# The first quarter of the MLP's up-projection as seven half-block products

## The chip, the core and the metric

The kernel runs on one core of a Trainium2 chip. The core has five engines with instruction queues of their own: TensorE (PE) multiplies matrices into PSUM, VectorE (DVE) and ScalarE (ACT) work elementwise, GpSimd (POOL) here mostly issues adding DMA transfers, and SyncE (SP) issues plain ones. The engines wait for one another by semaphores. The metric is the device time of one execution in microseconds; less is better.

## What is computed

The reference is a residual block: three token mixers on one normalised input, an output projection with a residual, and an MLP. Only the end of the output projection and the MLP matter here (512 tokens, 1024 channels, 4096 hidden channels, all float32):

```
x = x + mixed @ w_out[l]
u = _rmsnorm(x, g_mlp[l]) @ w_ff1[l]
x = x + jnp.square(jax.nn.relu(u)) @ w_ff2[l]
```

The hidden channels are worked off in four quarters of 1024. For each quarter the kernel makes the up-projection (1024 x 1024 weights), squares the positive part, and adds the down-projection of that quarter onto x.

## The kernel before

**Number format.** A product in float32 is made of three passes of a faster format. `w_pair` (L71) splits a block of weights of 128 x 1024 into a high part `whi` on ScalarE (L77) and a low part `wlo` on VectorE (L78), which is the block less the high part. There are four buffers of each, so four blocks can be held split. The other operand is split likewise. Each step is then three matmuls: high x high, high x low, low x high (L87 to L89, L170 to L172, L197 to L199).

**Two ways to multiply.** A plain product of a 1024 x 1024 block with 512 tokens is made of 8 output columns of 128, each of 8 k-steps with three matmuls 512 wide. The other way is a Strassen-like scheme: weights and activations are cut in halves in both directions, and seven products of half blocks are made in place of eight. For it, sums of half blocks are needed: those of the weights are made by adding DMA transfers (`w_more`, L204, issued by POOL) and by one add on VectorE (L1331); those of the activations by VectorE. The seven results are added up into the four quadrants of the output on ScalarE and VectorE. In the up-projection a half product is `product_f` (L186): two blocks of weights, 48 matmuls that are 256 wide. In the output and down-projections it is `product` (L161), with matmuls 512 wide.

**Before the change** the output projection (`out_proj`), the down-projections and quarters 1 to 3 of the up-projection (`ff1`) are made the second way, and quarter 0 (`ff1_0`) the first way, from an array of its own, `w_ff1a`, in the layout for columns.

**Where quarter 0 stands.** In `out_proj` the last product d is accompanied by the transposes of the first four tiles of x1 (`u_tile` 0 to 3). `u_tile` transposes 4 x 128x128 into a bank `tr` (two of these), then ScalarE makes the high part (L97), VectorE the low part (L98), and ScalarE a float32 copy U (L1149). Tiles 4 to 7 need the second half of x1, which is only whole when product d has been added on. `ff1_0` starts columns 0 and 1 on k-steps 0 to 3, does tiles 4 to 7 meanwhile, then goes on with the other k-steps and columns. Between them stands `u_forms` (L1169): the sums S3, S5, S6 and S4 of the activations and their splits, which quarters 1 to 3 use. `norm1` works out the scale of the norm, which is applied behind the down-projection. `end(0)` and `end(1)` load the first blocks of the down-projection and split its first operands.

**Order.** The program is written in one order, and a scheduler puts the instructions of each engine in a queue: the earliest in the program that is ready goes first. Buffers of one tag are given out in the order of the program. The tags that matter: `whi`/`wlo` (4 each), `raw` (3 blocks, loaded from the SP queue), `rq` (4 blocks: weights of the other scheme, and U), `h` (8 tiles, each as large as a block; in `out_proj` they hold the split operands `sp...`), `S` (one buffer), `mix` and `gate` (8 each), PSUM banks `pj` (2), `q4` (4), `tr` (2).

Of the kernel before, what the change touches and what calls it, by code (L numbers as in the profile page):

```python
# [8 lines left out]
F32 = mybir.dt.float32  # L9
# [3 lines left out]
ALU = mybir.AluOpType  # L13
# [21 lines left out]
@with_exitstack  # L35
def tile_block(ctx: ExitStack, tc: tile.TileContext, xT, x_, memT, mem_, small,
               w_sbqk, w_mlqk, w_vo, w_if, w_gate, w_kv,
               w_proj, w_out, w_ff1a, w_ff1, w_ff2, out_):
    nc = tc.nc
    act, dve, pe, pool = nc.scalar, nc.vector, nc.tensor, nc.gpsimd  # L40
    act.preload_act_table_set("natural_log_exp_and_others")
# [7 lines left out]
    def f32(ap):  # L49
        return ap.bitcast(F32)  # L50
# [17 lines left out]
    def mix(name="mix"):  # L68
        return hp.tile([P, T], F32, tag="mix", bufs=NK, name=name)

    def w_pair(raw, parts=1, before=lambda i: None):  # L71
        hi = wp.tile([P, W], F32R, tag="whi", bufs=4, name="whi")
        lo = wp.tile([P, W], F32R, tag="wlo", bufs=4, name="wlo")
        for i in range(parts):
            c = slice(i * W // parts, (i + 1) * W // parts)
            before(i)
            act.activation(out=hi[:, c], in_=raw[:, c], func=AF.Copy)  # L77
            dve.tensor_tensor(out=lo[:, c], in0=raw[:, c], in1=f32(hi[:, c]), op=ALU.subtract)  # L78
        return hi, lo

    def load_w(src):
# [4 lines left out]
    def mm3(out, lh, ll, rh, rl, start, stop):  # L86
        pe.matmul(out, lh, rh, start=start, stop=False)  # L87
        pe.matmul(out, lh, rl, start=False, stop=False)  # L88
        pe.matmul(out, ll, rh, start=False, stop=stop)  # L89
# [111 lines left out]
    def w_more(raws, w, fh, kh):  # L201

        for v in range(2):
            pool.dma_start(out=raws[v], in_=w[fh, 2 * kh + v], accum_op=ALU.add)  # L204

    def w_pairs(raws):
        return [w_pair(raw) for raw in raws]


    sm = cp.tile([P, NSM], F32, tag="sm", name="sm")  # L210
# [868 lines left out]
    def w_raw(w, fh, kh):  # L1079

        raws = [fpool.tile([P, W], F32, tag="rq", bufs=4, name="rq") for v in range(2)]
        for v in range(2):
            nc.sync.dma_start(out=raws[v], in_=w[fh, 2 * kh + v])
        return raws

    def w_raw2(w, fh, kh):

        raws = [wp.tile([P, W], F32, tag="raw", bufs=3, name="rq2") for v in range(2)]
        for v in range(2):
            nc.sync.dma_start(out=raws[v], in_=w[fh, 2 * kh + v])  # L1090
        return raws
# [35 lines left out]
    def x1_add(th, fh, src, op, final=False):  # L1127
        for j in range(2):
            i = 2 * th + j
            dve.tensor_tensor(out=x1[i][fh], in0=x1[i][fh], in1=src[j], op=op)  # L1130
            if final:
                sq = tmp("sq")
                act.activation(out=sq, in_=x1[i][fh], func=AF.Square, accum_out=ssq[:, fh, i:i + 1])
# [59 lines left out]

    def f_first(qt):

        F11 = w_raw(w_ff1[qt - 1], 0, 0)
        F3 = w_raw2(w_ff1[qt - 1], 1, 1)
        w_more(F3, w_ff1[qt - 1], 1, 0)
        first["F"] = F11, F3

    def out_proj():

        B11, B3, sp11, sp3 = (early[n] for n in ("B11", "B3", "sp11", "sp3"))
        a, c, d, b = [pj(), pj()], [q4(), q4()], [q4(), q4()], [tr(), tr()]
        w11 = w_pairs(B11)
        w3 = w_pairs(B3)

        product(a, sp11, w11, True, False)
        w_more(B11, w_out, 1, 0)
        S = stile("S5")  # L1210
# [24 lines left out]
        product(a, sp12, w21, False, True)  # L1235
        sp22 = s_of(1, 1)
        sp4 = s_form(S, ALU.subtract, lambda k: S[:, k], lambda k: mA(1, 0, k))
        w4 = w_pairs(B3)
        for j in range(2):
            dve.tensor_tensor(out=V[j], in0=V[j], in1=b[j], op=ALU.subtract)  # L1240

        product(c, sp22, w4, False, True)
        w22 = w_pairs(B22)
        x1_add(0, 0, a, ALU.add, True)
        x1_add(1, 0, V, ALU.add)

# [12 lines left out]
        act.activation(out=s, in_=o, func=AF.Relu, scale=scale)  # L1259
        act.activation(out=out, in_=s.rearrange("p (a b) -> p a b", a=2), func=AF.Square)  # L1260

    def ff1_plain(f, w, o, ks):
        hi, lo = w
        for k in ks:
            mm3(o, hi[:, k * P:(k + 1) * P], lo[:, k * P:(k + 1) * P], u[k][:, 0, :], u[k][:, 1, :],
                k == 0, k == NK - 1)

    def ff1_0(R, end):

        def out(f, o):  # L1270
            s = tmp("rs")
            act.activation(out=s, in_=o, func=AF.Relu)
            act.activation(out=R[f // 4][:, f % 4, :], in_=s, func=AF.Square)

        ws, os = [], []
        for f in range(2):
            ws.append(load_w(w_ff1a[f]))
            os.append(pj())
            ff1_plain(f, ws[f], os[f], range(4))
            u_tile(4 + 2 * f)  # L1280
            u_tile(5 + 2 * f)
        norm1()
        for f in range(2):
            ff1_plain(f, ws[f], os[f], range(4, NK))
            out(f, os[f])
        for f in range(2, NK):
            if f < 5:
                u_forms(f - 2)
            if f == 6:
                end(0)  # L1290
            o = q4()
            ff1_plain(f, load_w(w_ff1a[f]), o, range(NK))
            out(f, o)
        u_forms(3)
        return end(1)

    def ff1(qt, R, end):

        def out(th, fh, j, src, scale=1.0):
            relu2(R[fh][:, 2 * j:2 * j + 2, 2 * th * P:2 * (th + 1) * P], src, scale)  # L1300

        F11, F3 = first["F"]
        G = w_ff1[qt - 1]
        a, c, d, e = [pj(), pj()], [q4(), q4()], [q4(), q4()], [tr(), tr()]
        w11 = first["w11"]
        w3 = w_pairs(F3)

        product_f(a, us["A11"], w11, True, False)
        w_more(F11, G, 1, 0)
        F21 = w_raw2(G, 0, 1)  # L1310
        V = [mix("V1") for j in range(2)]
        X = [mix("X1") for j in range(2)]
        for j in range(2):
            act.activation(out=V[j], in_=a[j], func=AF.Copy)
        w5 = w_pairs(F11)

        product_f(c, us["S3"], w3, True, False)
        w_more(F11, G, 1, 1)
        w21 = w_pairs(F21)
        for j in range(2):  # L1320
            act.activation(out=X[j], in_=c[j], func=AF.Copy)

        product_f(d, us["S5"], w5, True, False)
        F22 = w_raw(G, 1, 1)
        w6 = w_pairs(F11)
        for j in range(2):
            dve.tensor_tensor(out=X[j], in0=X[j], in1=d[j], op=ALU.add)

        product_f(a, us["A12"], w21, False, True)
        for v in range(2):  # L1330
            dve.tensor_tensor(out=F11[v], in0=F11[v], in1=F21[v], op=ALU.add)  # L1331
        w4 = w_pairs(F11)
        for j in range(2):
            out(0, 0, j, a[j])

        product_f(e, us["S6"], w6, True, True)
        w22 = w_pairs(F22)
        for j in range(2):
            dve.tensor_tensor(out=V[j], in0=V[j], in1=e[j], op=ALU.subtract)
            dve.tensor_tensor(out=X[j], in0=X[j], in1=V[j], op=ALU.add)  # L1340
            out(1, 1, j, X[j], -1.0)

        product_f(c, us["A22"], w4, False, True)
        got = end(0)
        for j in range(2):
            t = tmp("fs")
            dve.tensor_tensor(out=t, in0=V[j], in1=c[j], op=ALU.add)
            out(1, 0, j, t)

        product_f(d, us["S4"], w22, False, True)  # L1350
        got += end(1)
        for j in range(2):
# [195 lines left out]
```

## Time and profile before

| what | value |
|---|---|
| median of three runs | 1114.66 us (1113.29 to 1115.28) |
| profiled execution, device time | 1113.77 us |
| its span, first to last instruction | 1112.0 us |
| granted TensorE clock | 1.0 of full speed throughout |
| stage of quarter 0, first transpose of x1 to first matmul of the down-projection | 785.12 to 835.92 us |
| quarter 1 of the up-projection, the other way | 874.00 to 914.04 us |

The profile is of one execution. A row of a group reads: line, engine, operation, what is written from what, shapes, count, then busy us and mean ns of one, then the idle time of the engine before these instructions and what ended it. A row of the timeline reads: start, duration, engine, line, operation, count, and in brackets the idle time before it with its cause. Durations of matmuls overlap, since they are pipelined: what one costs is the distance between starts. Device time and span differ by what lies before the first and after the last instruction, 1.77 us here.

### The profile page before, as it was taken

Reading aid. Unit: us, or ns where it says so; the run is one execution under the profiler, and the core shown is the slowest. Engines: PE = TensorE matmul, PEld = TensorE weight load, DVE = VectorE, ACT = ScalarE, POOL = GpSimd, SP = SyncE. Lnnn points to the kernel's source line nnn. Section 1 sums busy time; section 2 is a strip of 40 time slices with the busy share of each in tenths; the row PEclk is TensorE's granted clock in tenths of the full one; section 3 lists DMA queues with packets and bytes.
Section 4 is the critical chain, followed back from the end, with each engine's and each line's share of the span. In section 5 each row is a group of like instructions: output and inputs, shape, how many; then the busy total and the mean of one; then the engine's idle time right before and its main releaser. Section 6 shows DMA issues by size and latency. Waiting matters only on the chain.

```text
span 1112.0 us, 16472 instructions
## 1 busy us (share of the span) xinstructions
PE 1104.6 (99%) x6080; PEld 955.5 (86%) x6080; DVE 861.1 (77%) x1268; ACT 727.3 (65%) x1210; POOL 129.7 (12%) x229
## 2 busy tenths in 40 slices
PE   9999999999999999999999999999999999999998
PEld 6788889999987888888888888888788998998997
DVE  5899777778767867577978798679758588688698
ACT  6666664658557967677869678535856475485573
POOL 0112211321101000000000000000011101111110
PEclk9999999999999999999999999999999999999999
DMA  9978889874612242326434221755397868778774
GB/s 355 362 202 237 256 216 275 232 225 144 227 39 72 81 145 74 110 85 208 148 94 138 80 93 58 209 140 126 115 245 164 213 185 218 177 201 223 175 186 114
DMA packets 62680, 190.31 MB, mean 171 GB/s; under 512 B 6788, under 2 KB 13572, under 8 KB 62600
## 3 DMA queue, kind: packets, MB, share of 16 engines
q1 hardware_dynamic: 46024, 131.38, 34.6%
q0 software_dynamic: 16288, 57.68, 25.3%
q8 instruction: 48, 0.79, 0.3%
q10 hardware_dynamic: 288, 0.20, 0.1%
q14 instruction: 32, 0.26, 0.1%
HBM read 172.45 MB, written 16.79 MB: 170 GB/s over the span
## 4 chain that ended last, share of the span: by engine, by line
PE 92%; DVE 3%; ACT 3%; DMA 1%; issue 1%; POOL 0%; ACTq 0%; DVEq 0%
PE pj L87 9%; PE pj L88 9%; PE pj L89 9%; PE q L170 5%; PE q L172 5%; PE q L171 5%; PE q L197 4%; PE q L198 4%; PE q L199 4%; PE q L87 3%; PE q L88 3%; PE q L89 3%; PE pj L171 3%; PE pj L170 3%; PE pj L172 3%; PE pj L198 2%
## 5 line engine op out<-in xcount | busy, mean ns | idle before, releaser
L77 ACT ACTIVATE whi<-rq 128x1024 fp32r<-128x1024 f32 x112 | 118.0, 1057 | 112.1 <-PE q L172 27.9
L78 DVE TENSOR_TENSOR wlo<-rq,whi 128x1024 fp32r<-128x1024 f32 x112 | 136.5, 1221 | 57.4 <-ACT whi L77 53.8
L77 ACT ACTIVATE whi<-B 128x1024 fp32r<-128x1024 f32 x84 | 88.6, 1058 | 74.8 <-PE q L198 16.5
L78 DVE TENSOR_TENSOR wlo<-B,whi 128x1024 fp32r<-128x1024 f32 x84 | 102.5, 1223 | 42.0 <-ACT whi L77 41.7
L87 PE MATMUL pj<-h,whi 128*128 128x512 f32 x304 | 120.8, 398 | 0.0
L89 PE MATMUL pj<-h,wlo 128*128 128x512 f32 x304 | 119.1, 392 | 0.0
L88 PE MATMUL pj<-h,whi 128*128 128x512 f32 x304 | 119.0, 391 | 0.0
L78 DVE TENSOR_TENSOR wlo<-raw,whi 128x1024 fp32r<-128x1024 f32 x72 | 87.9, 1221 | 33.9 <-ACT whi L77 33.6
L77 ACT ACTIVATE whi<-raw 128x1024 fp32r<-128x1024 f32 x72 | 75.9, 1055 | 47.8 <-PE pj L88 34.8
L170 PE MATMUL q<-whi,shi 128*128 128x512 f32 (+1 forms) x232 | 89.9, 388 | 0.0
L172 PE MATMUL q<-whi,slo 128*128 128x512 f32 (+1 forms) x232 | 89.8, 387 | 0.0
L171 PE MATMUL q<-wlo,shi 128*128 128x512 f32 (+1 forms) x232 | 89.8, 387 | 0.0
L204 POOL DMA_DIRECT2D rq<-in_w_ff_dram x50 | 43.0, 897 | 283.3 <-DVE wlo L78 160.0
L87 PE MATMUL pj<-y,whi 128*128 128x512 f32 x192 | 75.7, 394 | 0.0
L89 PE MATMUL pj<-y,wlo 128*128 128x512 f32 x192 | 75.0, 391 | 0.0
L88 PE MATMUL pj<-y,whi 128*128 128x512 f32 x192 | 74.9, 390 | 0.0
L89 PEld LDWEIGHTS pj<-h,wlo 128*128 128x128 f32 x304 | 57.1, 188 | 11.9
L87 PEld LDWEIGHTS pj<-h,whi 128*128 128x128 f32 x304 | 57.1, 188 | 10.9
L88 PEld LDWEIGHTS pj<-h,whi 128*128 128x128 f32 x304 | 57.2, 188 | 10.8
L172 PEld LDWEIGHTS q<-whi,slo 128*128 128x128 f32 x232 | 43.6, 188 | 8.9
L171 PEld LDWEIGHTS q<-wlo,shi 128*128 128x128 f32 x232 | 43.6, 188 | 8.9
L170 PEld LDWEIGHTS q<-whi,shi 128*128 128x128 f32 x232 | 43.6, 188 | 8.8
(443 smaller groups left out, 3220.8 us busy)
## 6 DMA issues: line engine op xcount, KB each, us to landing
rq<-in_w_ff_dram SPq DMA_DIRECT2D x56, 512.0 KB, 5.4
rq<-in_w_ff_dram POOLq DMA_DIRECT2D x50, 512.0 KB, 5.7
B<-in_w_vo_dram SPq DMA_DIRECT2D x48, 512.0 KB, 5.9
B<-in_w_vo_dram POOLq DMA_DIRECT2D x24, 512.0 KB, 6.9
raw<-in_w_proj_dram SPq DMA_DIRECT2D x24, 512.0 KB, 3.5
raw<-in_w_sbqk_dram SPq DMA_DIRECT2D x16, 512.0 KB, 3.9
raw<-in_w_mlqk_dram SPq DMA_DIRECT2D x16, 512.0 KB, 3.5
rawk<-in_w_kv_dram SPq DMA_DIRECT2D x14, 512.0 KB, 8.2
```

Source lines behind the costliest of these rows:

```text
L77: act.activation(out=hi[:, c], in_=raw[:, c], func=AF.Copy)
L78: dve.tensor_tensor(out=lo[:, c], in0=raw[:, c], in1=f32(hi[:, c]), op=ALU.subtract)
L87: pe.matmul(out, lh, rh, start=start, stop=False)
L88: pe.matmul(out, lh, rl, start=False, stop=False)
L89: pe.matmul(out, ll, rh, start=False, stop=stop)
L170: pe.matmul(o[:, c], lh, w[0][:, cw], start=st, stop=False, **mm)
L171: pe.matmul(o[:, c], lh, w[1][:, cw], start=False, stop=False, **mm)
L172: pe.matmul(o[:, c], ll, w[0][:, cw], start=False, stop=sp_, **mm)
L197: pe.matmul(o, wh, uh, start=start and k == 0 and f % 2 == 0, stop=False, **mm)
L198: pe.matmul(o, wh, ul, start=False, stop=False, **mm)
L199: pe.matmul(o, wl, uh, start=False, stop=stop and k == 3, **mm)
L204: pool.dma_start(out=raws[v], in_=w[fh, 2 * kh + v], accum_op=ALU.add)
```

## The change

`ff1_0` is written anew in the second way, with seven products in this order: 1 (bank a, weights w11, tokens' first half, u tiles 0 to 3), 2 (onto a, w21, tiles 4 to 7), 3 (c, w3 with S3), 4 (d, w5 with S5), 5 (onto c, w4, the four-fold sum of weights), 6 (e, w6 with S6), 7 (onto d, w22 with S4). Tiles 4 to 7 are transposed behind product 1. The results are put together in V and X, two copies of a and two of c on ScalarE, ten adds on VectorE. All low parts are made on VectorE (the new parameter `low` keeps its default).

The weights come from `w_ff1[0]`, which now holds all four quarters (so the index of the others moves by one). `first_loads`, called in `out_proj` behind the split of its last block, issues most loads: F4, F3 and F21 into tiles of tag `h`, F11 into `raw`, and the adding transfers on POOL in the order of use. F22 is loaded into `h` in `ff1_0`, and a last addition onto F11 is issued there. `w_ff1a` and `ff1_plain` are gone.

```diff
+    def first_loads():
+        G = w_ff1[0]
+        def half(fh, kh):
+            raws = [hp.tile([P, W], F32, tag="h", bufs=NK, name="hq") for v in range(2)]
+            for v in range(2):
+                nc.sync.dma_start(out=raws[v], in_=G[fh, 2 * kh + v])
+            return raws
+        F4 = half(0, 1)
+        w_more(F4, G, 0, 0)
+        F11 = w_raw2(G, 0, 0)
+        F3 = half(1, 1)
+        w_more(F3, G, 1, 0)
+        F21 = half(0, 1)
+        w_more(F4, G, 1, 0)
+        w11 = w_pairs(F11)
+        w_more(F11, G, 1, 0)
+        w_more(F4, G, 1, 1)
+        first["F"] = w11, F11, F4, F21, F3, lambda: half(1, 1)
...
         product(c, sp22, w4, False, True)
         w22 = w_pairs(B22)
+        first_loads()
...
     def ff1_0(R, end):
-        ws, os = [], []
-        for f in range(2):
-            ws.append(load_w(w_ff1a[f]))
-            os.append(pj())
-            ff1_plain(f, ws[f], os[f], range(4))
-            u_tile(4 + 2 * f)
-            u_tile(5 + 2 * f)
-        norm1()
-        for f in range(2):
-            ff1_plain(f, ws[f], os[f], range(4, NK))
-            out(f, os[f])
-        for f in range(2, NK):
-            if f < 5:
-                u_forms(f - 2)
-            if f == 6:
-                end(0)
-            o = q4()
-            ff1_plain(f, load_w(w_ff1a[f]), o, range(NK))
-            out(f, o)
-        u_forms(3)
-        return end(1)
+        w11, F11, F4, F21, F3, more = first["F"]
+        a, c, d = [pj(), pj()], [q4(), q4()], [q4(), q4()]
+        product_f(a, u_of(0, 0), w11, True, False)
+        for f in range(4, NK):
+            u_tile(f)
+        V = [mix("V1") for j in range(2)]
+        X = [mix("X1") for j in range(2)]
+        for j in range(2):
+            act.activation(out=V[j], in_=a[j], func=AF.Copy)
+        w21 = w_pairs(F21)
+        F22 = more()
+        product_f(a, u_of(1, 0), w21, False, True)
+        u_forms(0)
+        w3 = w_pairs(F3)
+        norm1()
+        for j in range(2):
+            out(0, 0, j, a[j])
+        product_f(c, us["S3"], w3, True, False)
+        u_forms(1)
+        w5 = w_pairs(F11)
+        w_more(F11, G, 1, 1)
+        for j in range(2):
+            act.activation(out=X[j], in_=c[j], func=AF.Copy)
+        product_f(d, us["S5"], w5, True, False)
+        w4 = w_pairs(F4)
+        u_forms(2)
+        product_f(c, u_of(1, 1), w4, False, True)
+        w6 = w_pairs(F11)
+        for j in range(2):
+            dve.tensor_tensor(out=X[j], in0=X[j], in1=d[j], op=ALU.add)
+        w22 = w_pairs(F22)
+        e = [tr(), tr()]
+        product_f(e, us["S6"], w6, True, True)
+        u_forms(3)
+        end(0)
+        for j in range(2):
+            dve.tensor_tensor(out=V[j], in0=V[j], in1=e[j], op=ALU.subtract)
+            t = tmp("fs")
+            dve.tensor_tensor(out=t, in0=V[j], in1=c[j], op=ALU.add)
+            out(1, 0, j, t)
+            dve.tensor_tensor(out=X[j], in0=X[j], in1=V[j], op=ALU.add)
+            out(1, 1, j, X[j], -1.0)
+        product_f(d, us["S4"], w22, False, True)
+        got = end(1)
+        for j in range(2):
+            t = tmp("fs")
+            dve.tensor_tensor(out=t, in0=V[j], in1=d[j], op=ALU.add)
+            out(0, 1, j, t, -1.0)
+        return got
```

More of the change, by code (lines that the diff above doesn't have):

```diff
@@ L37, in tile_block @@
                w_sbqk, w_mlqk, w_vo, w_if, w_gate, w_kv,
-               w_proj, w_out, w_ff1a, w_ff1, w_ff2, out_):
+               w_proj, w_out, w_ff1, w_ff2, out_):
     nc = tc.nc
@@ L69, in mix, with w_pair @@
         return hp.tile([P, T], F32, tag="mix", bufs=NK, name=name)
-    def w_pair(raw, parts=1, before=lambda i: None):
+    def w_pair(raw, parts=1, before=lambda i: None, low=dve):
         hi = wp.tile([P, W], F32R, tag="whi", bufs=4, name="whi")
@@ L77, in w_pair @@
             act.activation(out=hi[:, c], in_=raw[:, c], func=AF.Copy)
-            dve.tensor_tensor(out=lo[:, c], in0=raw[:, c], in1=f32(hi[:, c]), op=ALU.subtract)
+            low.tensor_tensor(out=lo[:, c], in0=raw[:, c], in1=f32(hi[:, c]), op=ALU.subtract)
         return hi, lo
@@ L204, in w_more, with w_pairs @@
             pool.dma_start(out=raws[v], in_=w[fh, 2 * kh + v], accum_op=ALU.add)
-    def w_pairs(raws):
-        return [w_pair(raw) for raw in raws]
+    def w_pairs(raws, low=dve):
+        return [w_pair(raw, low=low) for raw in raws]
     sm = cp.tile([P, NSM], F32, tag="sm", name="sm")
@@ L1194, in f_first @@
     def f_first(qt):
-        F11 = w_raw(w_ff1[qt - 1], 0, 0)
-        F3 = w_raw2(w_ff1[qt - 1], 1, 1)
-        w_more(F3, w_ff1[qt - 1], 1, 0)
+        F11 = w_raw(w_ff1[qt], 0, 0)
+        F3 = w_raw2(w_ff1[qt], 1, 1)
+        w_more(F3, w_ff1[qt], 1, 0)
         first["F"] = F11, F3
+    def first_loads():
[16 more added lines that the diff above has]
+        first["F"] = w11, F11, F4, F21, F3, lambda: half(1, 1)
     def out_proj():
@@ L1260, in relu2, with out @@
         act.activation(out=out, in_=s.rearrange("p (a b) -> p a b", a=2), func=AF.Square)
[L1262 to L1266, printed above, removed]
-    def ff1_0(R, end):
[L1270 to L1273, printed above, removed]
-        ws, os = [], []
-        for f in range(2):
-            ws.append(load_w(w_ff1a[f]))
-            os.append(pj())
-            ff1_plain(f, ws[f], os[f], range(4))
-            u_tile(4 + 2 * f)
-            u_tile(5 + 2 * f)
-        norm1()
-        for f in range(2):
-            ff1_plain(f, ws[f], os[f], range(4, NK))
-            out(f, os[f])
-        for f in range(2, NK):
-            if f < 5:
-                u_forms(f - 2)
-            if f == 6:
-                end(0)
-            o = q4()
-            ff1_plain(f, load_w(w_ff1a[f]), o, range(NK))
-            out(f, o)
-        u_forms(3)
-        return end(1)
+    def ff1_0(R, end):
+        def out(th, fh, j, src, scale=1.0):
+            relu2(R[fh][:, 2 * j:2 * j + 2, 2 * th * P:2 * (th + 1) * P], src, scale)
+        w11, F11, F4, F21, F3, more = first["F"]
+        G = w_ff1[0]
+        a, c, d = [pj(), pj()], [q4(), q4()], [q4(), q4()]
[11 more added lines that the diff above has]
+        w3 = w_pairs(F3)
+        norm1()
+        for j in range(2):
[16 more added lines that the diff above has]
+        product_f(e, us["S6"], w6, True, True)
+        u_forms(3)
+        end(0)
[13 more added lines that the diff above has]
+        return got
@@ L1302, in ff1 @@
         F11, F3 = first["F"]
-        G = w_ff1[qt - 1]
+        G = w_ff1[qt]
         a, c, d, e = [pj(), pj()], [q4(), q4()], [q4(), q4()], [tr(), tr()]
@@ L1534 @@
         "w_out": wide(a["w_out"][0]),
-        "w_ff1a": cols(a["w_ff1"][0][:, :D])[0],
-        "w_ff1": np.stack([wide(a["w_ff1"][0][:, i:i + D]) for i in range(D, 4 * D, D)]),
+        "w_ff1": np.stack([wide(a["w_ff1"][0][:, i:i + D]) for i in range(0, 4 * D, D)]),
         "w_ff2": np.stack([wide(a["w_ff2"][0][i:i + D]) for i in range(0, 4 * D, D)]),
```

## The prediction

> **What bounds the kernel now.** I read the page from the top, then the stage that the change touches. The page's first part and its chain of work say whether TensorE sets the time.
>
> ```profile
> span 1112.0 us, 16472 instructions
> PE 1104.6 (99%) x6080; PEld 955.5 (86%) x6080; DVE 861.1 (77%) x1268; ACT 727.3 (65%) x1210; POOL 129.7 (12%) x229
> PEclk9999999999999999999999999999999999999999
> PE 92%; DVE 3%; ACT 3%; DMA 1%; issue 1%; POOL 0%; ACTq 0%; DVEq 0%
> ```
>
> The chain is 92% matmul, at a granted clock that never drops. So a change pays by the matmul time that it takes off TensorE's stream, less the idle time that it opens there. Over the whole span VectorE is at 77% and ScalarE at 65%, but these are averages, so I cut out the stage. Its borders are found in the timeline of TensorE (columns: start us, us, engine, line, operation): first transpose of x1, first matmul of the plain quarter, first matmul of the down-projection.
>
> ```profile
> 785.12 1.03 PE L1145 MATMUL tr<-ident,x 128*128 128x128 f32 x8
> 785.91 0.48 PE L170 MATMUL q<-whi,shi 128*128 128x512 f32 x1
> ...
> 788.72 0.39 PE L87 MATMUL pj<-x1g,whi 128*128 128x512 f32 x1
> ...
> 803.50 0.39 PE L88 MATMUL q<-x1g,whi 128*128 128x512 f32 x1
> ...
> 835.92 0.39 PE L170 MATMUL pj<-whi,shi 128*128 128x512 f32 x1
> ```
>
> The view by windows has a row for each part, and the last one is the same work done in the new way: quarter 1, which already runs as seven half-block products (first matmul at 874.00, the next stage's at 914.04).
>
> ```profile
> 785.12:788.72 3.60, 3.60 (x21) 3.13 (x20) 2.27 (x3) 2.56 (x4) 0.00 (x0) 1.00 0.51 158
> 788.72:803.50 14.78, 14.77 (x74) 11.32 (x73) 11.77 (x24) 13.94 (x28) 0.00 (x0) 1.00 0.22 70
> 803.50:835.92 32.42, 32.42 (x145) 26.85 (x143) 18.06 (x20) 18.88 (x29) 4.32 (x5) 1.00 0.85 226
> 874.00:914.04 40.04, 40.04 (x337) 40.04 (x336) 27.35 (x29) 25.31 (x32) 5.13 (x6) 1.00 0.76 188
> 785.00:836.00 51.00, 50.99 (x239) 41.40 (x238) 32.10 (x45) 35.46 (x59) 4.32 (x5) 1.00 0.64 176
> 846.00:860.00 14.00, 14.00 (x64) 11.59 (x63) 13.93 (x15) 7.50 (x8) 2.58 (x3) 1.00 0.93 193
> ...
> 874.00 0.28 PE L197 MATMUL pj<-x1g,whi 128*128 128x256 f32 x1
> ...
> 914.04 0.40 PE L170 MATMUL pj<-whi,shi 128*128 128x512 f32 x1
> ```
>
> Columns: window, us, then busy us and instructions of PE, weight load, VectorE, ScalarE, POOL, clock, DMA share, GB/s. From 803.50 on TensorE is the limit, with VectorE and ScalarE at 56% and 58%. In the 14.78 us before that ScalarE is busy 13.94, or 94%: there the transposed tiles are drained, split and copied. That is the place to watch.
>
> **The matmul stream.** Removed: 8 columns x 8 k x 3 = 192 matmuls 512 wide. From 803.50 to 835.92 143 of them take 32.42, 0.2267 us each, so 192 are 43.53 us. Added: 7 products x 48 = 336 matmuls 256 wide; the quarter-1 row shows 336 in 40.04 us, 0.1192 each. Difference: **-3.49 us**. Half the width costs more than half the time (0.1192 against 0.1133), so of the eighth that seven products save in columns, 5.4 us, over a third is lost. The 32 transposes stay; eight take 0.79 us (785.12 to 785.91), 0.099 each.
>
> The page "TensorE: Matmul & The Clock Gate" of the Trainium skill, section Back-to-back issue gap, speaks against the change: in a stream of weight load and matmul pairs the spacing is set by both, about 81 ns at 128 columns and 131 ns at 512. On a straight line between these, an estimate from that page, 256 columns cost 98 ns, and 336 x 98 - 192 x 131 is a loss of 7.7 us. The trace does not agree: 227 ns at 512, 119 ns at 256, a gain of 3.5.
>
> **The start of the stage.** Before, 788.72 to 803.50 holds 49 matmuls (11.11) and 24 transposes (2.37), so 1.30 us are idle. After, the same place holds products 1 and 2 (96 x 0.1192 = 11.44) and the same transposes: 13.81, which would end at 802.53. Product 1 needs u tiles 0 to 3 only, product 2 needs 4 to 7, product 3 the split difference S3 and the pair w3. Before, TensorE could also work on columns whose pairs were all converted in advance, as four buffers hold four columns; now four buffers hold two products. What ScalarE did last there, and what it now has to do in addition:
>
> ```profile
> 771.51 0.39 PE L170 MATMUL pj<-whi,shi 128*128 128x512 f32 x1
> ...
> 782.39 0.39 PE L170 MATMUL q<-whi,shi 128*128 128x512 f32 x1
> ...
> 785.36 1.06 ACT L77 ACTIVATE whi<-raw 128x1024 fp32r<-128x1024 f32 x1 [0.44 <-ACT sq L1133]
> ...
> 800.87 1.35 ACT L1149 ACTIVATE U<-tr,sm 128x512 f32<-128x512 f32 x2 [0.24 <-DVE x1g L98]
> 802.34 1.06 ACT L77 ACTIVATE whi<-raw 128x1024 fp32r<-128x1024 f32 x1
> ...
> L1314 ACT ACTIVATE V<-pj 128x512 f32<-128x512 f32 x2 | 1.2, 588 | 0.5 <-PE pj L199 0.5
> ...
> L1260 ACT ACTIVATE R<-rs 128x512 f32<-128x512 f32 x8 | 4.9, 622 | 0.1
> L1340 DVE TENSOR_TENSOR X<-X,V 128x512 f32<-128x512 f32 x2 | 1.3, 682 | 0.0
> ...
> L1149 ACT ACTIVATE U<-tr,sm 128x512 f32<-128x512 f32 x8 | 5.4, 693 | 1.0 <-DVE x1g L98 1.0
> L78 DVE TENSOR_TENSOR wlo<-raw,whi 128x1024 fp32r<-128x1024 f32 x6 | 7.3, 1223 | 3.9 <-ACT whi L77 3.8
> ...
> L197 PEld LDWEIGHTS pj<-x1g,whi 128*128 128x128 f32 x96 | 18.4, 191 | 0.1
> L204 POOL DMA_DIRECT2D rq<-in_w_ff_dram x50 | 43.0, 897 | 283.3 <-DVE wlo L78 160.0
> ...
> rq<-in_w_ff_dram SPq DMA_DIRECT2D x56, 512.0 KB, 5.4
> rq<-in_w_ff_dram POOLq DMA_DIRECT2D x50, 512.0 KB, 5.7
> ```
>
> ScalarE's queue ends with the last U copies at 802.22; the conversion at 802.34 is that of column 4 and falls away. New before product 3: (a) two copies V of product 1's banks, 2 x 0.59 = 1.18; product 2 adds onto these banks, so it must wait for them. (b) Block w21 is loaded into tiles of tag h, and its two are released only when product c of the output projection is done (product d's first matmul, 782.39). With 5.4 us to landing that is 787.8, so the slot at 785.36, in which column 2 was converted, stays empty, and one conversion of 1.06 moves into the full stretch. (c) The first w3 conversion, 1.06. Together 3.30 us: 802.22 + 3.30 = 805.5 for w3's high part, and 1.22 later, 806.7, VectorE has the low part, which the third matmul of product 3 reads. Some of the 0.84 us that ScalarE idles in that stretch can be filled. Bounds: no delay beyond the 1.30 before, if the copies and conversions slip into gaps; or all of it, product 3 at 806.5. I take **805.9**, nearer the upper bound, as ScalarE is already at 94%. That is 3.4 us idle against 1.30, **+2.1 us**.
>
> Behind the V copies in ScalarE's queue stand the drains of u tiles 6 and 7, which product 2's second half reads; that wait is inside the 3.4. If x1 or a transposed tile comes later by t, all of this moves by t.
>
> **Products 3 to 7.** 240 x 0.1192 = 28.61. ScalarE has some 26 us to do in these 29 (eleven conversions, the splits of S5, S6, S4, A11, two X copies, six outputs of two passes) and VectorE some 25. The tightest is product 4: after 805.5 ScalarE does the second w3 half, the two outputs of bank a (4 x 0.6, as L1260), the S5 split and a w5 half, 1.06 + 2.4 + 1.06 + 1.06, so the high part at 811.1 and the low at 812.3, where product 4 is due at 805.9 + 5.72 = 811.6. I count **+0.3 us**; below is 0, above 1.5 if VectorE is late too. Products 5 to 7 have 2 us and more. Into the down-projection VectorE has S3, its split and w3's low parts to do within the first product; quarters 1 to 3 do the same at their ends, and no idle time of TensorE stands at 914.04. Zero, with +1.5 as the upper end.
>
> **Transfers.** Per 512 KB the queue rows give 1.54 us of all DMA engines for a plain transfer and 2.56 for an adding one:
>
> ```profile
> q1 hardware_dynamic: 46024, 131.38, 34.6%
> q0 software_dynamic: 16288, 57.68, 25.3%
> ```
>
> (0.524/131.38 x 0.346 x 1112, and likewise.) Removed are 8 plain ones (12.3 us), added 10 plain and 12 adding (46.1), over 768 to 820, a stretch whose DMA share was 0.51, then 0.22, then 0.85 with the down-projection's loads in it. It fits. The longest chain, block F4 with three additions, begins at about 771.5, when product b ends (product a's first matmul, 771.51), and takes 5.4 + 3 x 5.7 = 22.5: 794 alone, needed at 813. POOL's queue holds the additions in the order in which their products come, and was empty there (no POOL work in either window up to 803.50). The last addition onto F11 follows w5's low part (812.3): 0.9 to issue (L204), 5.7 to land, 819, two conversion steps, 821; product 6 is due at 823.4. Zero, and 2 us if landing doubles.
>
> **Sum.** -3.49 + 2.1 + 0.3 = **-1.1 us**. The profiled execution took 1113.77 (its span 1112.0 and 1.77 around it), so 1112.7 there; the median of the three runs is 0.9 above it, and against that I predict 1113.6.
>
> **The rivals.**
> - *The start is hidden.* ScalarE fits copies and conversions into gaps, idle time stays at 1.30: the whole 3.49 is gained, **1111.2**. For it: the U copies waited 1.0 us for VectorE's low part of the same tile, time that a conversion can use. Against: 94%.
> - *VectorE becomes the bound* (the other side). In 785 to 836 it works 32.10; six more low parts (6 x 1.22, as L78) and ten adds of 0.68 (as L1340) make 46.2, since all low parts lie on VectorE. With nothing idle that is less than the stage. The stage now is 50.80, so it decides from an occupancy of 91% down: at 85%, as each low part waits for its high part first, 54.4, +3.6, **1118.3**. For it: in 788.72 to 803.50 VectorE reached 80%. Against: at 846 to 860 it reached 13.93 of 14.
> - *Late blocks.* w21 or the last F11 lands 2 to 3 us later because the queue is fuller: the gain is eaten, **1115**.
> - *The narrow matmuls do not stream.* The change would then not do what it says. If each waited for its own weight load (L197, 191 ns), 336 would take 64.2 us, +20.7, **1135**. The row of 40.04 with 336 loads in it speaks against it. By the rule of the Trainium skill's page named above it would be 1114.66 + 7.7, some 1122, an estimate.
>
> **How the numbers follow.** Forecast 0.50 (own range 1112.2 to 1115.2), hidden start 0.24, VectorE 0.17, late blocks 0.07, narrow matmuls 0.02. A measurement of this kernel can tell about 0.2%, 2.2 us, from no change: faster means below 1112.4, slower above 1116.9. Faster: 0.22 of the hidden start and 0.06 of the forecast. Slower: 0.15 of VectorE, 0.01 of late blocks, 0.02 of narrow matmuls. The range leaves out the slower end of VectorE and the best end of the hidden start (which with fewer waits than before could reach 1110.5): 1110.8 to 1117.8.
>
> **What would show it.** Right: 336 more matmuls of 256 columns with starts 0.119 apart; idle time of PE's weight load in the first 18 us of the stage, ended by ScalarE or VectorE, summing to about 3; product 3 near 805.9 and the down-projection 1.1 us nearer to the first transpose. Wrong: waits of the weight load on low parts (L78) in products 4 to 7 (VectorE), conversions waiting for DMA (late blocks), or a gap before the down-projection.

## The result, and the profile after

| | before | after |
|---|---|---|
| median (range, runs) | 1114.22 us (1113.29 to 1115.34, 6) | 1123.59 us (1121.87 to 1126.31, 6) |
| ratio, 95% interval | | 1.0085 (1.0071 to 1.0099) |
| profiled execution, its span | 1113.77, 1112.0 | 1121.87, 1120.1 |
| stage of quarter 0 | 785.12 to 835.92, 50.80 us | 784.83 to 842.42, 57.59 us |

The change makes the kernel slower by 9.4 us, beyond the upper end of the range. The page of the changed kernel, its parts on busy time, clock and chain:

```profile
span 1120.1 us, 16822 instructions
PE 1104.2 (99%) x6224; PEld 963.1 (86%) x6224; DVE 873.3 (78%) x1284; ACT 733.8 (66%) x1220; POOL 140.1 (13%) x241
PEclk9999999999999999999999999999899999999999
PE 90%; DVE 4%; ACT 3%; DMA 2%; issue 1%; POOL 0%; SPq 0%; ACTq 0%; DVEq 0%
```

TensorE is as busy as before (1104.2 us against 1104.6), the span is 8.1 longer, and the clock row, 9 in every slice before, has an 8 in one slice. The view by windows shows the stage in three pieces and then quarter 1 (window, us, busy us and instructions of PE, weight load, VectorE, ScalarE, POOL, then clock, DMA share, GB/s):

```profile
784.83:795.37 10.54, 3.77 (x21) 2.94 (x19) 3.82 (x5) 4.03 (x9) 5.25 (x6) 0.89 1.05 311
795.37:812.10 16.73, 15.70 (x108) 14.91 (x109) 12.14 (x17) 15.11 (x28) 1.70 (x2) 0.86 1.06 230
812.10:842.42 30.32, 30.32 (x254) 30.32 (x254) 26.96 (x39) 22.21 (x34) 5.96 (x7) 1.00 0.92 220
880.53:920.83 40.30, 40.30 (x338) 40.30 (x336) 27.39 (x29) 25.32 (x32) 5.11 (x6) 1.00 0.74 183
```

In the first 10.54 us TensorE works 3.77, and VectorE and ScalarE some 4: they wait, while the DMA engines are full (1.05). From 812.10 to the down-projection TensorE has no pause. The last row is a second, small loss: quarter 1 takes 40.30 where it took 40.04, and quarters 2 and 3 likewise. The timeline of the changed kernel tells what was waited for. ScalarE:

```profile
785.93 1.24 ACT L97 ACTIVATE x1g<-tr,sm 128x512 fp32r<-128x512 f32 x2
793.69 1.06 ACT L77 ACTIVATE whi<-hq 128x1024 fp32r<-128x1024 f32 x1 [6.51 <-DMA hq<-in_w_ff_dram]
794.65 1.25 ACT L1149 ACTIVATE U<-tr,sm 128x512 f32<-128x512 f32 x2
```

TensorE:

```profile
795.37 1.97 PE L1145 MATMUL tr<-ident,x 128*128 128x128 f32 x8 [6.77 <-ACT U L1149]
```

SyncE's issues (four of 512 KB; the first two, at 782.08, are block F21 for w21, the others, at 788.41, F22), and VectorE's low parts of u tiles 0 and 1:

```profile
782.08 7.19 SPq L1208 DMA_DIRECT2D hq<-in_w_ff_dram  x4
```

```profile
786.63 1.41 DVE L98 SCALAR_TENSOR_TENSOR x1g<-tr,sm,x1g 128x512 fp32r<-128x512 f32 x2 [0.57 <-ACT x1g L97]
```

These are to be read from the last to the first. Transposes of u tiles 2 and 3 need the two banks `tr`, which the U copies of tiles 0 and 1 set free. The high parts of these tiles were made by 787.2 and the low parts by 788.0, but the U copies stand in ScalarE's queue behind the first conversion of w21, and that waits for its block, issued at 782.08 and there only at 793.6: 11.5 us for 512 KB. ScalarE keeps to the order of its queue here: it is idle for 6.51 us, and two copies of 0.6 us, for which all was ready by 788.0, begin at 794.65, behind a transfer that they don't use.

Why the block was so late stands in the table of issues (the last figure is the median time in us from issue to landing, for 765 to 830) and in the windows of the changed kernel:

```profile
hq<-in_w_ff_dram SPq DMA_DIRECT2D x8, 512.0 KB, 11.1
hq<-in_w_ff_dram POOLq DMA_DIRECT2D x8, 512.0 KB, 12.2
```

```profile
776.00:780.00 4.00, 4.00 (x19) 3.34 (x18) 4.00 (x6) 2.65 (x6) 1.70 (x2) 1.00 0.55 156
780.00:784.00 4.00, 4.00 (x20) 3.30 (x19) 2.91 (x4) 0.96 (x2) 0.00 (x0) 1.00 1.04 266
784.00:788.00 4.00, 4.00 (x24) 3.39 (x23) 2.60 (x4) 3.17 (x7) 0.68 (x1) 1.00 1.05 272
788.00:792.00 4.00, 0.60 (x3) 0.18 (x1) 0.63 (x2) 0.00 (x0) 1.33 (x4) 1.00 1.03 373
792.00:796.00 4.00, 0.63 (x3) 0.63 (x4) 1.23 (x2) 2.31 (x4) 3.24 (x4) 0.64 1.06 277
796.00:800.00 4.00, 4.00 (x21) 4.00 (x20) 2.83 (x5) 3.81 (x9) 0.91 (x2) 0.50 1.05 274
...
808.00:812.00 4.00, 3.99 (x34) 3.70 (x33) 3.43 (x5) 3.80 (x8) 0.00 (x0) 1.00 1.06 211
```

And the kernel before, in three of the same windows:

```profile
780.00:784.00 4.00, 4.00 (x20) 3.30 (x19) 3.46 (x6) 2.34 (x3) 0.00 (x0) 1.00 0.69 185
784.00:788.00 4.00, 4.00 (x23) 3.43 (x22) 2.51 (x3) 3.14 (x7) 0.00 (x0) 1.00 0.65 223
788.00:792.00 4.00, 3.99 (x20) 2.68 (x20) 3.85 (x6) 3.44 (x7) 0.00 (x0) 1.00 0.42 133
```

The DMA engines are full, a share of 1.03 or more, from 780 to 812, where they had room before. The bytes moved per second fall meanwhile to 211 GB/s, as at the end nearly all that runs is adding (from 804 to 812 the queue of the adding transfers has 106.3% of the engines' time, that of the plain ones 0.2%). And in the two windows after the pause the granted clock is 0.64 and 0.50: from 795.37 to 799.9 TensorE works at half speed, its matmuls of product 1 starting 0.21 us apart, and 0.12 from there on. (The Trainium skill, "TensorE: Matmul & The Clock Gate", part 1 on the HAM clock gate, has the clock at half after an idle window of some 3.4 us; the 0.64 and 0.50 behind a wait of 6.8 us agree. In e7_plain below the clock is at half behind a wait of 2.46 us, which does not agree; there the measurement decides.)

The sum of the stage: with nothing idle it would be 3.60 for the end of the output projection with the first eight transposes (as in the kernel before), 2.37 for the other 24 transposes and 336 x 0.1199 = 40.29, together 46.26. It took 57.59, so 11.3 are lost: 6.8 in the wait; about 2.2 in the half clock (795.37 to 804.14 holds eight transposes and product 1, 6.55 us of work, and takes 8.77); some 2.3 in short waits and starts. Before, by the same count, 1.3 were lost.

### The profile page after: what moved, and what is told of

The parts are those of the page before. It is cut to its first block, busy times and chain, and to the rows that moved or that the text cites. A ratio compares the mean times of both kernels' runs of the same rounds, so it can differ in the third digit from the quotient of the medians.

```text
span 1120.1 us, 16822 instructions
## 1 busy us (share of the span) xinstructions
PE 1104.2 (99%) x6224; PEld 963.1 (86%) x6224; DVE 873.3 (78%) x1284; ACT 733.8 (66%) x1220; POOL 140.1 (13%) x241
## 4 chain that ended last, share of the span: by engine, by line
PE 90%; DVE 4%; ACT 3%; DMA 2%; issue 1%; POOL 0%; SPq 0%; ACTq 0%; DVEq 0%
PE pj L87 9%; PE pj L88 9%; PE pj L89 9%; PE q L171 5%; PE q L170 5%; PE q L172 5%; PE q L197 5%; PE q L198 5%; PE q L199 5%; PE pj L171 3%; PE pj L170 3%; PE pj L172 3%; PE pj L198 2%; PE pj L197 2%; PE pj L199 2%; PE q L87 2%
## 5 line engine op out<-in xcount | busy, mean ns | idle before, releaser
L77 ACT ACTIVATE whi<-rq 128x1024 fp32r<-128x1024 f32 x118 | 124.2, 1056 | 110.7 <-DMA rq<-in_w_ff_dram 37.9
L78 DVE TENSOR_TENSOR wlo<-rq,whi 128x1024 fp32r<-128x1024 f32 x118 | 143.8, 1220 | 48.5 <-ACT whi L77 48.2
L78 DVE TENSOR_TENSOR wlo<-raw,whi 128x1024 fp32r<-128x1024 f32 x64 | 78.0, 1221 | 29.5 <-ACT whi L77 29.3
L77 ACT ACTIVATE whi<-raw 128x1024 fp32r<-128x1024 f32 x64 | 67.4, 1055 | 42.2 <-PE pj L88 36.0
L204 POOL DMA_DIRECT2D rq<-in_w_ff_dram x54 | 47.9, 936 | 252.7 <-DVE wlo L78 174.5
```

The costliest lines, as they stand in the source:

```text
L78: low.tensor_tensor(out=lo[:, c], in0=raw[:, c], in1=f32(hi[:, c]), op=ALU.subtract)
```

## The experiments

The theories. **A**: the adding transfers fill the DMA engines, blocks land late, and a conversion that waits for one holds up ScalarE's queue. **B**: ScalarE has too much to do at the start of the stage (the prediction's reason for its +2.1). **C**: VectorE is the bound. Ratios are to the kernel before, measured beside each.

**Loads in the order of need** (e1_need).

```diff
-        F4 = half(0, 1)
-        w_more(F4, G, 0, 0)
+        F21 = half(0, 1)
         F11 = w_raw2(G, 0, 0)
         F3 = half(1, 1)
         w_more(F3, G, 1, 0)
-        F21 = half(0, 1)
-        w_more(F4, G, 1, 0)
+        F4 = half(0, 1)
+        w_more(F4, G, 0, 0)
         w11 = w_pairs(F11)
         w_more(F11, G, 1, 0)
+        w_more(F4, G, 1, 0)
         w_more(F4, G, 1, 1)
```

> The loads of first_loads in the order in which their products come: F21 first (into the two tiles of h that come free at about 771), then F11 and F3, and F4 last with its three additions. Nothing is left out. Theory A (the first conversion of w21 stands in ScalarE's queue ahead of the copies U0 and U1 and waits there for a transfer that the full DMA queues land 11.6 us after its issue): F21 lands before 780, the wait of 6.5 us and the slow clock after it go, 1114 to 1115.5, about 8 to 9 us less than the changed kernel. Theory B (ScalarE has too much work at the start, whatever lands): under 3 us less, 1120 or more. Theory C (VectorE is the bound): no difference. If F4's additions then land after 815, product 5 waits and up to 5 us of the gain are given back.

Measured: 1121.98 us, ratio 1.007 (1.0055 to 1.0085), 1.6 less than the changed kernel. A had given 1114 to 1115.5, and up to 5 more if product 5 waits; by the number alone B and C come nearer. The trace decides: w21's conversions no longer wait, TensorE works 13.31 of the 14.10 us from 785.90 to 800.00, and another wait has taken the place of the first. ScalarE's timeline, and the window in which it falls:

```profile
816.11 1.06 ACT L77 ACTIVATE whi<-hq 128x1024 fp32r<-128x1024 f32 x1 [5.51 <-DMA hq<-in_w_ff_dram]
821.15 1.06 ACT L77 ACTIVATE whi<-hq 128x1024 fp32r<-128x1024 f32 x1 [3.50 <-DMA hq<-in_w_ff_dram]
```

```profile
816.00:824.00 8.00, 5.48 (x38) 4.67 (x37) 2.98 (x4) 3.55 (x4) 0.00 (x0) 0.97 1.04 215
```

Now F4 is last, and w4 waits for its additions; the DMA share is still over 1.0, and the blocks of the down-projection behind it are late too, so that this stage takes 41.44 us in place of 38.1. The order mostly chooses who waits.

**The w21 conversions behind the U copies** in ScalarE's queue (e2_queue).

```diff
-        w21 = w_pairs(F21)
+        with tc.issue_after(copies[3]):
+            w21 = w_pairs(F21)
```

> The loads as in the changed kernel; the two conversions of w21 are put behind the copy U3 in ScalarE's queue (order of issue alone, no further wait). Nothing is left out. Theory A in its form 'the place in the queue': transposes 2 and 3 and product 1 no longer wait though F21 lands as late as before (793 to 794), 1114.5 to 1116.5. Theory A in its form 'TensorE needs the block itself by then': product 2 waits for it instead, 3 us or less of gain, 1120. Theory B: ScalarE's idle 6.5 us are used, but the start still ends 3 us later than product times alone, 1114 to 1117. Theory C: no difference.

Measured: 1120.39 us, 1.0054 (1.0039 to 1.0069). A's value for the place in the queue was 1114.5 to 1116.5; 3.2 of the 9.4 us come back, no more. The head of the queue is another, and it is the same wait. ScalarE's timeline:

```profile
790.24 1.06 ACT L77 ACTIVATE whi<-rq 128x1024 fp32r<-128x1024 f32 x1 [7.12 <-DMA rq<-in_w_ff_dram]
```

This conversion is that of w11's second block, without which product 1 can't be finished; behind it in the queue stand the drains and U copies of tiles 0 and 1. TensorE's wait for these copies is 3.63 us in place of 6.77.

**The adding transfers left out** (e3_noadd): the six calls of `w_more` for quarter 0, so its sums of weights aren't made.

> The six adding calls of quarter 0 are left out, so products 3 to 6 multiply plain blocks; all else as in the changed kernel, ScalarE's order too. Theory A with full DMA queues as the cause of the late landing: F21 lands 5 to 6 us after its issue at 782, at about 788, ScalarE waits under 1.5 us, 1114 to 1116.5. If instead the late release of the tiles alone is the cause: landing stays near 793 and the time near 1123. Theories B and C: additions don't load these engines, no difference.

Measured: 1114.58 us, 1.0001 (0.9992 to 1.0011): as fast as before. Issues, windows and TensorE's only waits in the stage:

```profile
hq<-in_w_ff_dram SPq DMA_DIRECT2D x8, 512.0 KB, 4.5
```

```profile
785.00:813.00 28.00, 26.89 (x208) 25.41 (x207) 22.73 (x34) 26.64 (x47) 0.00 (x0) 1.00 0.25 85
813.00:835.00 22.00, 22.00 (x182) 21.87 (x181) 20.18 (x27) 14.43 (x22) 4.32 (x5) 1.00 0.87 209
```

```profile
797.52 0.38 PE L197 MATMUL pj<-x1g,whi 128*128 128x256 f32 x1 [0.43 <-ACT x1g L97]
798.59 0.38 PE L197 MATMUL pj<-x1g,whi 128*128 128x256 f32 x1 [0.68 <-ACT V L1295]
```

The twelve transfers cost 1123.59 - 1114.58 = **9.0 us**, practically the whole loss, though they are no part of TensorE's work. It also prices the rest of the change: ScalarE is busy 26.64 of 28 us, 95%, and yet TensorE is idle only 1.11 there. The stage takes 48.42 us (785.72 to 834.14), 2.4 less than before. In the profiled executions the slower quarters (below) take back 0.8 of that, the first and the last down-projection 0.6, and the time ahead of the stage 0.6. Nor is it the late release of F21's tiles that makes the block late: it is issued no earlier here (782.96), and its first conversion begins at 787.54 without a wait.

**Both orders at once** (e4_both): e1_need and e2_queue together.

> Both edits together: F21 first, F4 last, and w21's conversions behind U3 in ScalarE's queue. Nothing is left out. Theory A: once F21 lands in time the place in the queue matters little, within 1 us of the run with the loads reordered, 1113.5 to 1115.5, and what is left over the sum of matmul times is theory B's part: with product 3 starting at 805 to 806 of the span as predicted, 1113.5; with no such rest, 1111.

Measured: 1124.09 us, 1.0087 (1.0067 to 1.0108), no better than the change alone, where A had given 1113.5 to 1115.5.

```profile
816.00:824.00 8.00, 5.03 (x33) 4.44 (x32) 3.63 (x4) 3.37 (x5) 0.00 (x0) 0.87 1.06 218
```

The start runs well, the down-projection is reached at 838.03 in place of 842.42, and the time is lost in products 5 and 6 and in the down-projection (41.89 us). The best of the three orders, e2_queue, wins 3.2 of the 9.4 us back; the runs that follow show that the DMA engines are short of time more than of order.

**What an adding transfer costs**: plain ones in their place, same bytes, tiles, queue and order, so that the sums of weights aren't made (e7_plain).

```diff
+        def again(raws, fh, kh):
+            for v in range(2):
+                pool.dma_start(out=raws[v], in_=G[fh, 2 * kh + v])
+
         F4 = half(0, 1)
-        w_more(F4, G, 0, 0)
+        again(F4, 0, 0)
...
```

> The twelve adding transfers become plain ones from the same source to the same tile, on POOL's queue and in the same order; the sums are left out, so the output is another. If the load of the engines is what counts (A: 1.54 us of all engines for a plain block against 2.56 for an adding one), 22 blocks cost 34 us in place of 46, the share falls below 1.0 from about 800 on, and the time is 1115 to 1119. If an adding transfer costs no more than a plain one, or if it is the order behind one another on the same tile, the time stays at 1121 to 1124.

Measured: 1118.21 us, 1.0034 (1.002 to 1.0047). One window of 20 us, first of this kernel, then of the changed one, then of the one without additions:

```profile
784.00:804.00 20.00, 16.52 (x106) 14.79 (x104) 12.55 (x17) 15.35 (x30) 4.23 (x8) 0.91 0.91 362
```

```profile
784.00:804.00 20.00, 13.23 (x80) 12.20 (x79) 9.39 (x13) 12.40 (x25) 6.96 (x8) 0.83 1.05 283
```

```profile
784.00:804.00 20.00, 18.89 (x138) 17.25 (x137) 16.03 (x22) 19.17 (x37) 0.00 (x0) 1.00 0.31 113
```

Full engines moved 362 GB/s over a share of 0.91 here, but 211 in the changed kernel's window at 808, where they mostly add: 512 KB in 1.3 us against 2.5 (0.524 MB over 0.362/0.91, and over 0.211). Of the 9.0 us, 3.6 come with the bytes alone (1118.21 - 1114.58) and 5.4 because they are added. TensorE's wait at the start is shorter here, and the clock is at half all the same (TensorE's timeline, and the window behind the wait):

```profile
791.37 1.24 PE L1145 MATMUL tr<-ident,x 128*128 128x128 f32 x8 [2.46 <-ACT U L1149]
```

```profile
792.00:796.00 4.00, 4.00 (x23) 4.00 (x23) 3.14 (x5) 4.00 (x11) 0.75 (x2) 0.58 1.02 414
```

**Only F4's three additions left out** (e8_nof4add), half of the twelve transfers; the sum for w4 isn't made.

> Only the three additions onto block F4 are left out (6 of the 12 adding transfers, 15.4 us of all engines), so w4 isn't the sum and the output is another. Full DMA engines (A): the stretch at a share of 1.0 ends some 15 us sooner; the blocks for w21 and w11 are issued behind fewer transfers, so most of the 9.0 us comes back: 1115 to 1118. If the additions onto F11 and F3 are the cause, 1120 or more.

Measured: 1118.59 us, 1.0041 (1.0026 to 1.0056): F4's additions are worth 5.0 us of the 9.0, which leaves 4.0 for the others. The upper end of what A gave (1115 to 1118) is just missed: even with half of them, the U copies of tiles 0 and 1 still wait behind w21's block, 3.4 us. It is a matter of load, of which F4 is the larger part, and of no single transfer.

**F4 given up, its sum made on VectorE** (e5_dveadd).

```diff
-        w4 = w_pairs(F4)
         u_forms(2)
+        for v in range(2):
+            dve.tensor_tensor(out=F11[v], in0=F11[v], in1=F22[v], op=ALU.add)
+        w6 = w_pairs(F11)
...
+        for v in range(2):
+            dve.tensor_tensor(out=F21[v], in0=F21[v], in1=F11[v], op=ALU.add)
...
+        product_f(e, us["S6"], w6, True, True)
+        w4 = w_pairs(F21)
...
```

w6 is w5's block plus F22, w4 is that plus F21; product 6 goes ahead of product 5, F21 is loaded first and F22 early. Two plain transfers and eight of the twelve adding ones are gone.

> Block F4 is given up: the sum for w6 is F11 + F22 and that for w4 is F21 + F11, both by four adds on VectorE; product 6 comes ahead of product 5. Two plain loads and eight of the twelve adding transfers fall away, about 3.1 + 20.5 us of all DMA engines. Full DMA engines (A): landing comes back to 5 or 6 us from 11.6, the share falls well below 1.0 in 784 to 812, no conversion waits for a block over 1 us, and the time is near that of the kernel without adding transfers, 1114.6 (1113.5 to 1115.5). VectorE (C): it gets 4 x 1.22 = 4.9 us more where it already worked 20.2 of 22 us (813 to 835 without adding transfers), TensorE waits for low parts in products 6 and 5, and the time is 1117 to 1119. ScalarE's start (B) gives no difference to the changed kernel, 1123.

Measured: 1114.09 us, 1.0 (0.9991 to 1.001): as A said, with nothing of the computation left out. Issues and windows:

```profile
hq<-in_w_ff_dram SPq DMA_DIRECT2D x6, 512.0 KB, 7.1
```

```profile
784.00:804.00 20.00, 19.06 (x142) 17.57 (x141) 15.72 (x21) 19.16 (x37) 1.76 (x2) 1.00 0.67 155
```

Landing is not back at 5 or 6 us, a miss, and the DMA share is still 1.03 to 1.07 up to 796. But F21 now is first and is there in time, and TensorE works 19.06 of these 20 us in place of 13.23. The order alone is not the reason, as e1_need loaded F21 first too. C's 1117 to 1119 didn't come, although VectorE got 4.9 us more.

**The same four adds on POOL** (e6_pooladd): `pool.tensor_tensor` in the two places.

> As the one before, but the four adds are made by POOL, which has nothing to do there. Full DMA engines (A): landing as there; VectorE keeps its load of the kernel without adding transfers, so 1114.6 if POOL adds a block in 2 us or so. From the row of POOL's 128x128 adds (0.5 to 0.7 us each) a 128x1024 add could take up to 5 us; then product 6 comes some 5 to 8 us late and the time is 1119 to 1123.

Measured: 1121.78 us, 1.0066 (1.0051 to 1.0081). POOL's timeline and then VectorE's:

```profile
806.07 2.86 POOL L1316 TENSOR_TENSOR rq<-rq,hq 128x1024 f32<-128x1024 f32 x1 [19.82 <-DVE r L119]
...
814.15 2.75 POOL L1316 TENSOR_TENSOR rq<-rq,hq 128x1024 f32<-128x1024 f32 x1 [2.76 <-DVE wlo L78]
```

```profile
806.57 2.37 DVE L120 TENSOR_TENSOR r<-r 128x4 f32<-128x4 f32 x1
...
813.99 3.46 DVE L1162 TENSOR_TENSOR Su<-Su,U 128x512 f32<-128x512 f32 x2
```

An add takes POOL 2.4 to 2.9 us, less than the 5 allowed for; the time lies in the range given (1119 to 1123), but for another reason. While POOL adds, VectorE's tiny 128x4 operation takes 2.37 us (0.16 in the kernel with VectorE's adds) and a pair of 128x512 adds 3.46 (1.29 there). So the low parts of S5 and S6 that VectorE makes come late, and TensorE waits for them:

```profile
812.99 0.38 PE L198 MATMUL q<-u,whi 128*128 128x256 f32 x1 [2.15 <-DVE u L95]
...
823.19 0.39 PE L198 MATMUL tr<-u,whi 128*128 128x256 f32 x1 [2.70 <-DVE u L95]
```

The stage takes 56.69 us in place of 49.14. That is a third reading, which neither expectation had. The Trainium skill, "SBUF — State Buffer", section on the two separate sides, says that VectorE with two SBUF inputs and a POOL operation that reads SBUF exclude each other for the whole instruction; VectorE's operation of 2.37 us, which ends at 808.94 where POOL's add ends at 808.93, agrees with it.

**The slower pace of quarters 1 to 3** (e9_pad, e11_before_pad). Quarter by quarter and product by product, three of the seven products had gone from 0.1183 to 0.1200 us a matmul: 3, 4 and 6, those whose activations lie in the tiles u. These lie 128 bytes lower in the changed kernel, since the small tile of the norm is given out behind them, no more before. So a tile of 128 bytes was put in front of them, once in e5_dveadd, which brings them back to the old addresses, and once in the kernel before, which moves them away.

```diff
+        pad = fpool.tile([P, 32], F32, tag="pad", name="pad")
+        pool.memset(pad, 0.0)
```

> The kernel with four adds on VectorE, and a 128-byte tile in front of the six tiles u (the split S3, S5 and S6), which puts these at the addresses that they have before the change. In the changed kernels they lie 128 bytes lower, as the small tile of the norm is now given out behind them. Address theory: products 3, 4 and 6 of quarters 1 to 3 come back to 0.1183 us a matmul from 0.1200, a quarter to 40.04 from 40.30 us, and the time falls by 0.8 us to 1113.3. If the pace comes from something else (the order of instructions, the banks), the quarters stay at 40.30 and the time at 1114.1.

> The kernel before the change, with the 128-byte tile in front of the tiles u, so that they lie 128 bytes higher; nothing else is moved but the small tile of the norm behind them. Address theory: quarters 1 to 3 take 40.30 us in place of 40.04, and the time rises by 0.8 us to 1115.2. If the address isn't it, 40.04 and no change.

Measured: 1113.73 us, 0.999 (0.9981 to 0.9998), and the kernel before with the tile 1116.15, 1.0014 (1.0006 to 1.0023). Quarter 1 in e5_dveadd, in e9_pad and in the kernel before with the tile:

```profile
872.13:912.43 40.30, 40.30 (x337) 40.30 (x336) 28.04 (x30) 24.06 (x32) 6.00 (x7) 1.00 0.81 196
```

```profile
873.83:913.88 40.05, 40.05 (x338) 40.05 (x337) 29.00 (x31) 24.98 (x32) 6.00 (x7) 1.00 0.84 199
```

```profile
875.78:916.08 40.30, 40.30 (x338) 40.30 (x336) 27.39 (x29) 25.33 (x32) 5.13 (x6) 1.00 0.81 190
```

The pace follows the address, in both directions. In time it is 0.25 us a quarter. The medians move by 0.4 and 1.9 us, where 0.8 was forecast for each. In the profiled executions, from the first transpose of x1 to the end of the span, e9_pad takes 325.3 us against 326.0 in e5_dveadd, and the kernel before 327.6 with the tile against 326.9: 0.8 less and 0.7 more, as forecast. The rest lies ahead of the first transpose there: it starts at 786.91 in the kernel before with the tile and at 785.12 without, and over the kernels of this document between 784.63 and 787.25. What that comes from was not followed. Why the one address is slower stays open too.

**The squares of x1 put later** (e10_squares), behind product 6, to relieve ScalarE at the start.

```diff
             if final:
-                sq = tmp("sq")
-                act.activation(out=sq, in_=x1[i][fh], func=AF.Square, accum_out=ssq[:, fh, i:i + 1])
+                squares.append((i, fh))
...
-        norm1()
...
         w4 = w_pairs(F21)
+        sums()
+        norm1()
```

> The one with the 128-byte tile, and the squares of x1 (eight passes of ScalarE, 0.62 + 0.19 us each, five of them at 791 to 795.4, ahead of the drains of tiles 4 to 7) with the norm that they feed put behind product 6, where ScalarE has time. ScalarE's start (B): TensorE's idle time in the first 20 us of the stage, about 2.9 us over the matmuls and transposes, falls by 1 to 1.5 us; 1111.8 to 1112.3. If the drains wait for x1 or VectorE instead, no difference to the one with the 128-byte tile alone.

Measured: 1113.37 us, 0.9995 (0.9987 to 1.0004), no clear gain over e9_pad where B had given 1111.8 to 1112.3, and widely spread (1111.69 to 1116.13). In the profiled execution, which is the slowest of the twelve, TensorE's timeline and a window show a new wait and a clock of 0.57 behind it:

```profile
799.69 0.38 PE L197 MATMUL pj<-x1g,whi 128*128 128x256 f32 x1 [1.32 <-ACT x1g L97]
...
800.76 0.38 PE L197 MATMUL pj<-x1g,whi 128*128 128x256 f32 x1 [0.68 <-ACT V L1305]
```

```profile
802.00:806.00 4.00, 4.00 (x24) 4.00 (x23) 3.11 (x4) 2.85 (x5) 0.00 (x0) 0.57 0.00 0
```

The scheduler had filled the room with a conversion of w3, at 798.01, ahead of the drains, at 798.97. Taking work off ScalarE did not by itself help; B in this form isn't borne out.

**VectorE's order ahead of product 6** (e12_order): in e9_pad the add that w6 needs is put before S6, and S4 behind w6.

```diff
-        u_forms(2)
         for v in range(2):
             dve.tensor_tensor(out=F11[v], in0=F11[v], in1=F22[v], op=ALU.add)
+        u_forms(2)
         w6 = w_pairs(F11)
+        s4_form()
```

> The kernel with four adds on VectorE and the 128-byte tile; the sum for w6 is made ahead of S6, and S4 behind w6. VectorE (C, here in one place): product 6 waits for VectorE, which works without a pause from 802 to 826, and two sums of 1.3 us stand ahead of the add that w6 needs. With that order changed the 0.7 us of idle at 818 to 822 (PE busy 3.31 of 4) go, and the time is 1112.9 to 1113.2, 0.6 to 0.8 below that without the new order. If something else holds product 6, no difference.

Measured: **1112.6 us, 0.9983 (0.9974 to 0.9992)**, the fastest of all, 1.7 parts in 1000 below the kernel before. Windows around the start of product 6, e9_pad and then e12_order:

```profile
818.00:822.00 4.00, 3.31 (x28) 3.12 (x27) 4.00 (x5) 1.74 (x2) 0.45 (x1) 1.00 0.96 368
```

```profile
816.00:820.00 4.00, 3.72 (x31) 3.52 (x31) 4.00 (x6) 1.34 (x4) 0.00 (x0) 1.00 0.84 302
```

The pause shrinks from 0.69 to 0.28 us, not to nothing. VectorE is at 4.00 of 4 in both, so here, and only here, C has a point: with four more adds VectorE sets the start of product 6. The stage as a whole gains just 0.1 (48.97 us against 49.08), and the executions of the two kernels overlap (1111.96 to 1114.86 and 1111.46 to 1113.52), so most of the 1.1 us between their medians is not shown to come from the order.

## Why the prediction was wrong

The kernel before, over the stretch that the paragraph on transfers names, 768 to 820:

```profile
768.00:820.00 52.00, 51.99 (x243) 42.24 (x242) 42.99 (x60) 37.27 (x62) 1.70 (x2) 1.00 0.49 164
```

- **Where it failed.** The step is the paragraph on transfers, "It fits", with its price of "Zero, and 2 us if landing doubles". Landing did double, from 5.4 to 11.1 us (median of the eight plain ones into `hq`), and the price was 9.0 us (e3_noadd). The amount of the additions was right: twelve transfers, at 2.56 us each. Three things were wrong. First, the sum was not made: by the row above the engines are busy for 0.49 of the 52 us, 25.5; less 12.3 and plus 46.1 that is 59.3, more than the stretch holds. Second, the transfers can't be spread over it: F21 could only be issued at 782.08, when its tiles came free, and was needed by 788, in the midst of the additions, and the engines were full from 780 to 812. Third, the price of a late block was taken as the delay of its own product, when the block's conversion stands in a queue in order. Nor are the additions in POOL's queue in the order of the products, as the paragraph and the section on the change have it: the first two, at 776.60 and 777.91, are F4's, for product 5.
- **The same step inside the start.** (b) let F21 land after 5.4 us, at 787.8, and charged "one conversion of 1.06" for that. It landed at 793.6, and the charge was 6.8 us of idle TensorE and 2.2 of half clock, since the U copies stood behind that conversion.
- **The rival "late blocks"** had the right mechanism, with w21 as its first example, at 1115 and a chance of 0.07. Its sign, conversions that wait for DMA, is what the timeline shows. It was mis-sized by the same error, 2 to 3 us of delay in place of some 6 (793.6 against 787.8), with nothing queued behind.
- **The matmul stream** was nearly right: 336 matmuls at 0.1199 us in place of 0.1192. Not foreseen was that the change would slow the other three quarters by the same 0.6%, 0.8 us in all, through an address (e9_pad).
- **The start's +2.1 and product 4's +0.3** were too high: without additions the stage loses 48.42 - 46.26 = 2.2 us against 1.3 before, so +0.9 in place of +2.4. "The start is hidden" was nearer, as long as blocks come in time: ScalarE at 95% kept pace.
- **VectorE the bound**: not so in the change. It worked 26.96 of the last 30.32 us, 89%, and TensorE never waited. It becomes so in one place with four more adds.
- **Narrow matmuls**: 40.30 us for 336, 120 ns each, speak once more against a wait for each weight load, and against the estimate from the Trainium skill ("TensorE: Matmul & The Clock Gate", Back-to-back issue gap).

So the forecast of 1113.6 comes near for the change without the additions (1114.58) and for the one with half of its sums on VectorE (1114.09); the transfers alone take the time out of the range. That it comes so near there is in part luck: the start cost 1.5 us less than forecast, and the other quarters lost 0.8 that nobody had counted.

## What to carry to other kernels

Sum up DMA time, with what runs there already, by the stretch between the first possible issue and the first need, not over the stage. Where the share came to 1.0 here, landing times doubled, and no order that was tried won back more than about a third of the loss. For each conversion that waits for a transfer, look at what stands behind it in its engine's queue: that, and not the block's own product, is the price of a late block, with the half clock of TensorE on top. A sum of weights that an engine with time to spare can make from blocks already loaded was better made there than by further adding transfers (e5_dveadd against the changed kernel).

## What the runs showed that was not expected

- An adding transfer of 512 KB takes about 2.5 us of all DMA engines, a plain one 1.3 when the engines are full: 211 against some 400 GB/s.
- Moving the activation tiles by 128 bytes changes the pace of their matmuls from 0.1183 to 0.1200 us, and back.
- POOL's elementwise add of 128x1024 takes 2.4 to 2.9 us and holds VectorE up nearly as long: 2.37 us for an operation of 0.16.
- A TensorE wait of 6.8 us costs some 2.2 us more in half clock afterwards, and a wait of 2.46 us is followed by half clock too (e7_plain).
- The profiled executions reach the first transpose of x1 at 784.63 to 787.25; that spread of 2.6 us is more than some of the differences followed here, so small ones are better read from that point on.
